# Gate and up of three feed-forwards as seven block products, with weight blocks summed by accumulating DMAs

## The chip, the cores and the metric

The kernel runs on one core of a Trainium2 chip. The metric is device time in microseconds (us), from the start of the program to its end; lower is better. The kernel before takes 2795.41 us (median of 3 runs, 2793.9 to 2799.13).

## What is computed

Two small transformer blocks, one after the other, on 512 tokens of width 1024, all in float32. The first has a hybrid mixer (sparse attention and an mLSTM), a cross-attention and a feed-forward (FFN 0). The second has two layers, each of half-step FFN, mixer, half-step FFN: FFN 1, a conformer convolution and FFN 2 in layer 0, then FFN 3, an attention and FFN 4 in layer 1. The change is in FFN 1, 2 and 4, which are, cut to what matters:

```python
D_MODEL, SEQ, D_FF_2 = 1024, 512, 2816
def swiglu_ffn_2(x, w_gate, w_up, w_down):
    return (jax.nn.silu(x @ w_gate) * (x @ w_up)) @ w_down
...
h = h + HALF_STEP * swiglu_ffn_2(rms_norm_2(h, ffn1_norm[layer]), ffn1_w_gate[layer], ...)
...
h = h + HALF_STEP * swiglu_ffn_2(rms_norm_2(h, ffn2_norm[layer]), ffn2_w_gate[layer], ...)
```

## The kernel before, in words

Activations lie transposed in SBUF, as 8 tiles `x[k]` of 128 features by 512 tokens. Every float32 operand of a large product is split in two float32r parts (`split`, L122): ACT copies it to a hi part (`whi`, `xh`, `hh`), DVE subtracts that to get a lo part (`wlo`, `xl`, `hl`). `mm3` (L170) then issues three matmuls for one 128 by 128 block of weights: hi by hi, hi of the weights by lo of the activations, lo of the weights by hi of the activations. So the third of three is the first that needs the weights' lo part. Each matmul loads its own weights.

`load_w` (L160) loads a 128 by 1024 weight tile by a DMA from SP into `wraw` (3 buffers) and splits it into `whi` and `wlo` (4 buffers each). A buffer of `whi` is free again when PE has done the product that used it.

`ffn` (L304) works in two halves of 11 tiles of F (128 of the 2816 hidden features). For each tile it makes gate and up, 8 blocks of weights times 3 matmuls of 512 tokens each (`projs`, L196), multiplies both by the row of inverse norms `rb`, and keeps silu(gate) times up as `hh`/`hl` (`up`, L308). After 11 tiles, `down` (L325) makes the 8 output tiles from them, and `cb` (L1030, in `half_ffn`, L1027) adds half of each to `x`. With `head=2` (of the three FFNs only FFN 1, before) the first two tiles of F are made in two token halves of 256 (`HALVES`), so that PE can start before all of `x` is normalised.

PSUM has 8 banks, handed out in turn by tag: `mm` 2, `sc` 3, `tr` 2, `po` 1. A scheduler orders the instructions of each engine when the program is built; the engines then work through their queues in that fixed order, each instruction waiting on semaphores for its inputs and its buffers. POOL does some sums of squares and nothing in the middle of an FFN; no DMA is issued on it.

Of the kernel before, what the change touches and what calls it, by code (L numbers as in the profile page):

```python
# [9 lines left out]
F32 = mybir.dt.float32  # L10
# [4 lines left out]
P = 128  # L15
# [10 lines left out]
NSA_H = 8  # L26
BUCKETS = 32
BW = 640
WHOLE = slice(0, S)
HALVES = (slice(0, S // 2), slice(S // 2, S))  # L30

# [17 lines left out]
def kernel(ctx: ExitStack, tc: tile.TileContext, t: dict, out: bass.AP):  # L49
# [9 lines left out]
    def nm(s):  # L59
        uid[0] += 1  # L60
        return f"{s}_{uid[0]}"
# [5 lines left out]
    def ps_tile(tag):  # L67
        return psum.tile([P, 512], F32, tag=tag, bufs=banks[tag], name=nm(tag))
# [5 lines left out]
    def mm_tile():  # L74
        return next_tile("mm")
# [39 lines left out]
    def v(name, j):  # L115
        o = VOFF[name] + j
        return vec[:, o : o + 1]
# [4 lines left out]
    def split(src, hi, lo, scale=None, pieces=1, hp=1):  # L122
        if scale is None:
            w = src.shape[-1] // hp
            for c in range(hp):
                sl = slice(c * w, (c + 1) * w) if hp > 1 else slice(None)
                last_hi[0] = nc.scalar.activation(hi[:, sl], src[:, sl], AF.Copy)  # L127
            w = src.shape[-1] // pieces
            for c in range(pieces):
                sl = slice(c * w, (c + 1) * w) if pieces > 1 else slice(None)  # L130
                nc.vector.tensor_tensor(lo[:, sl], src[:, sl], f32(hi[:, sl]), ALU.subtract)  # L131
        else:
            nc.scalar.activation(hi, src, AF.Copy, scale=scale)
            nc.vector.scalar_tensor_tensor(lo, src, scale, f32(hi), ALU.mult, ALU.subtract)  # L134
# [25 lines left out]
    def load_w(ap, width, raw=None, pieces=1, hp=1):  # L160

        if raw is None:
            raw = wp.tile([P, width], F32, tag="wraw", bufs=3, name=nm("wraw"))
            nc.sync.dma_start(raw, ap)
        hi = wp.tile([P, width], F32R, tag="whi", bufs=4, name=nm("whi"))
        lo = wp.tile([P, width], F32R, tag="wlo", bufs=4, name=nm("wlo"))
        split(raw, hi, lo, pieces=pieces, hp=hp)
        return hi, lo

    def mm3(ps, lh, ll, rh, rl, start, stop):  # L170
        nc.tensor.matmul(ps, lh, rh, start=start, stop=False)  # L171
        nc.tensor.matmul(ps, lh, rl, start=False, stop=False)  # L172
        nc.tensor.matmul(ps, ll, rh, start=False, stop=stop)  # L173


    chain = []
# [2 lines left out]
    def tick():  # L179
        if chain:  # L180
            chain[0][0] -= 1
            if chain[0][0] == 0:
                chain.pop(0)[1]()

    def order_pe():
        pe_order.enter_context(tc.manual_schedule(engines={mybir.EngineType.PE}))

    def free_pe():
        while chain:
            chain.pop(0)[1]()  # L190
        pe_order.close()
# [4 lines left out]
    def projs(sets, xs, ts):  # L196
        for k in range(KT):
            sl = slice(k * P, (k + 1) * P)
            for ps, (hi, lo) in sets:
                mm3(ps[:, ts], hi[:, sl], lo[:, sl], xs[k][0][:, ts], xs[k][1][:, ts], k == 0, k == KT - 1)  # L200
                tick()
# [17 lines left out]

    def inv_rms(state, eps=1e-6, ts=WHOLE, psum_only=False):  # L220

        if not state:
            for j in range(KT):
                square_acc(x[j], j, state, eng=nc.vector)
        sums = rms_sums(state, eps, ts)
        rt, pb = rms_rows(sums, ts)
        if psum_only:
            return rt, pb
        rb = act_p.tile([P, S], F32, tag="rb", bufs=2, name=nm("rb"))[:, : ts.stop - ts.start]
        nc.vector.tensor_copy(rb, pb)  # L230
        return rt, rb

    def inv_rms_chain(state, first, second):

        if not state:
            for j in range(KT):
                square_acc(x[j], j, state, eng=nc.vector)
        got = []

        def finish():  # L240
            rt, pb = rms_rows(got[0], WHOLE)
            rb = act_p.tile([P, S], F32, tag="rb", bufs=2, name=nm("rb"))
            nc.vector.tensor_copy(rb, pb)
            got[:] = [rt, rb]

        chain.append([first, lambda: got.append(rms_sums(state, 1e-6, WHOLE))])
        chain.append([second, finish])
        return got
# [55 lines left out]
    def ffn(fp, xs, st, wg, wu, wd, out_cb, head=0, tail=0, step=None):  # L304


        r = []

        def up(p, pg, pu):
            if not r:  # L310
                r.append(inv_rms(st)[1])
            rb = r[0]
            gr = fp.tile([P, S], F32, tag="gr", bufs=2, name=nm("gr"))
            nc.vector.tensor_tensor(gr, pg, rb, ALU.mult)
            nc.scalar.activation(gr, gr, AF.Silu)
            su = fp.tile([P, S], F32, tag="su", bufs=2, name=nm("su"))
            nc.vector.tensor_tensor(su, pu, rb, ALU.mult)  # L317
            nc.vector.tensor_tensor(su, su, gr, ALU.mult)
            hh = fp.tile([P, S], F32R, tag=f"hh{p}", name=nm("hh"))
            hl = fp.tile([P, S], F32R, tag=f"hl{p}", name=nm("hl"))  # L320
            split(su, hh, hl)
            return hh, hl

        def down(half, n, ws, pd, h, ts=WHOLE):
            for k in range(FH):  # L325
                hi, lo = ws[k // 6]
                sl = slice(k % 6 * P, (k % 6 + 1) * P)
                mm3(pd[:, ts], hi[:, sl], lo[:, sl], h[k][0][:, ts], h[k][1][:, ts], k == 0, k == FH - 1)
                tick()

        for half in range(2):
            h = []
            nh = 0 if half else head
            ws = [[load_w(w[n], D, pieces=4) for w in (wg, wu)] for n in range(nh)]
            pss = [(mm_tile(), mm_tile()) for n in range(nh)]
            for ts in HALVES:
                for n in range(nh):
                    projs(list(zip(pss[n], ws[n])), xs, ts)
            free_pe()
            if nh:  # L340
                order_pe()
                got = inv_rms_chain(st, 4, 6)
                pss.append(tuple(at_tile() for _ in range(2)))
                for ps, w in zip(pss[nh], (wg, wu)):
                    proj(ps, load_w(w[nh], D), xs)
                free_pe()
                r.append(got[1])
            for p in range(FH):
                n = half * FH + p
                if p < len(pss):  # L350
                    pg, pu = pss[p]
                else:
                    g = load_w(wg[n], D)
                    u = load_w(wu[n], D)
                    pg = mm_tile()
                    proj(pg, g, xs)
                    pu = at_tile()
                    proj(pu, u, xs)
                h.append(up(p, pg, pu))

            def load_down(n):
                return [load_w(wd[half, n][:, a * P : b * P], (b - a) * P) for a, b in ((0, 6), (6, FH))]

            nt = tail if half else 0
            for n in range(KT - nt):
                pd = mm_tile() if n % 2 else at_tile()
                down(half, n, load_down(n), pd, h)
                out_cb(half, n, pd, WHOLE)
            ws = {n: load_down(n) for n in range(KT - nt, KT)}
            pds = {n: mm_tile() if n % 2 else at_tile() for n in ws}  # L370
            if nt:
                order_pe()
            for ts in HALVES:
                for n in ws:
                    down(half, n, ws[n], pds[n], h, ts)
                    out_cb(half, n, pds[n], ts)
                if nt and step:
                    step(ts)

# [647 lines left out]
    def half_ffn(xs, st, idx, nxt, head=0, tail=0, step=None, ap=False):  # L1027
        st2, xs2 = {}, []

        def cb(half, n, ps, ts):  # L1030
            last_add[0] = nc.vector.scalar_tensor_tensor(x[n][:, ts], ps[:, ts], 0.5, x[n][:, ts], ALU.mult, ALU.add)
            if half == 1:
                if nxt is not None:
                    xs2.append(split_x(n, nxt))
                square_acc(x[n], n, st2, ts, ap)

        with tc.tile_pool(name=f"fp{idx}", bufs=1) as fp:
            ffn(fp, xs, st, t[f"wg{idx}"], t[f"wu{idx}"], t[f"wd{idx}"], cb, head, tail,
                step and (lambda ts: step(st2, ts)))
        return xs2, st2  # L1040

    xs, st = half_ffn(xs, st, 1, "mix_norm_0", head=2)


    rt, rb = inv_rms(st)
    cs = ExitStack()
    cp = cs.enter_context(tc.tile_pool(name="cp", bufs=1))
# [466 lines left out]
```

## Time and profile before

| what | value |
|---|---|
| median of 3 runs | 2795.41 us |
| the profiled execution, its own time | 2799.96 us |
| its span, first to last instruction | 2798.2 us |
| busy: PE, DVE, ACT, POOL | 98%, 52%, 38%, 12% |
| mean granted TensorE clock | 0.994 |

"Busy" is the share of the span in which the engine works on at least one instruction. Matmuls overlap in the pipeline, so the time that one costs is read from the step between the starts of two, not from its own duration. A row of the timeline has the start, the duration, the engine, the source line and the operation with output and inputs; in brackets stands the idle time before it and what ended that.

### The profile page before, as it was taken

Reading aid. Unit: us, or ns where it says so; the run is one execution under the profiler, and the core shown is the slowest. Engines: PE = TensorE matmul, PEld = TensorE weight load, DVE = VectorE, ACT = ScalarE, POOL = GpSimd, SP = SyncE. Lnnn points to the kernel's source line nnn. Section 1 sums busy time; section 2 is a strip of 40 time slices with the busy share of each in tenths; the row PEclk is TensorE's granted clock in tenths of the full one; section 3 lists DMA queues with packets and bytes.
Section 4 is the critical chain, followed back from the end, with each engine's and each line's share of the span. In section 5 each row is a group of like instructions: output and inputs, shape, how many; then the busy total and the mean of one; then the engine's idle time right before and its main releaser. Section 6 shows DMA issues by size and latency. Waiting matters only on the chain.

```text
span 2798.2 us, 35182 instructions
## 1 busy us (share of the span) xinstructions
PE 2731.0 (98%) x13750; PEld 2252.2 (80%) x13750; DVE 1465.1 (52%) x2270; ACT 1074.5 (38%) x1772; POOL 339.0 (12%) x451
## 2 busy tenths in 40 slices
PE   8999999999999999999899999999999997999998
PEld 6877988888888888885788888898888874788887
DVE  7666564643436434449754344534444489543443
ACT  5676544422334323331333233343223366332223
POOL 0133132200002000012210000100000136200001
PEclk9999999999999999999999999999999999999999
DMA  5312321223222233236332322323232320222322
GB/s 194 105 46 99 114 76 53 93 85 109 98 83 92 91 99 103 82 110 171 83 113 87 102 98 85 111 84 104 82 109 89 107 65 4 83 96 85 107 84 81
DMA packets 86923, 263.19 MB, mean 94 GB/s; under 512 B 9655, under 2 KB 13751, under 8 KB 86756
## 3 DMA queue, kind: packets, MB, share of 16 engines
q1 hardware_dynamic: 85148, 258.42, 29.6%
q10 hardware_dynamic: 1608, 2.52, 0.3%
q8 instruction: 108, 1.77, 0.3%
q14 instruction: 59, 0.48, 0.1%
HBM read 256.60 MB, written 4.30 MB: 93 GB/s over the span
## 4 chain that ended last, share of the span: by engine, by line
PE 79%; DVE 4%; issue 1%; DMA 1%; ACT 1%; POOL 0%; SPq 0%; DVEq 0%; ACTq 0%
PE sc L171 9%; PE sc L172 9%; PE sc L173 9%; PE mm L172 7%; PE mm L173 7%; PE mm L171 7%; PE tr L171 6%; PE tr L172 6%; PE tr L173 6%; PE po L171 3%; PE po L172 3%; PE po L173 3%; DVE wlo L131 1%; PE po L1311 1%; DVE c L1114 1%
## 5 line engine op out<-in xcount | busy, mean ns | idle before, releaser
L127 ACT ACTIVATE whi<-wraw 128x1024 fp32r<-128x1024 f32 (+3 forms) x518 | 492.3, 955 | 1287.4 <-PE sc L172 430.7
L131 DVE TENSOR_TENSOR wlo<-wraw,whi 128x1024 fp32r<-128x1024 f32 (+4 forms) x559 | 581.1, 1049 | 384.4 <-ACT whi L127 383.1
L171 PE MATMUL mm<-xh,whi 128*128 128x512 f32 (+1 forms) x760 | 287.7, 379 | 6.3 <-ACT whi L127 5.9
L172 PE MATMUL mm<-xl,whi 128*128 128x512 f32 (+1 forms) x760 | 286.9, 377 | 5.5 <-DVE xl L134 5.5
L173 PE MATMUL mm<-xh,wlo 128*128 128x512 f32 (+1 forms) x760 | 286.4, 377 | 0.0
L171 PE MATMUL sc<-xh,whi 128*128 128x512 f32 (+1 forms) x696 | 270.1, 388 | 0.0
L172 PE MATMUL sc<-xl,whi 128*128 128x512 f32 (+1 forms) x696 | 269.2, 387 | 0.0
L173 PE MATMUL sc<-xh,wlo 128*128 128x512 f32 (+1 forms) x696 | 269.2, 387 | 0.0
L172 PE MATMUL tr<-xl,whi 128*128 128x512 f32 (+1 forms) x592 | 222.8, 376 | 3.1 <-DVE xl L134 3.1
L171 PE MATMUL tr<-xh,whi 128*128 128x512 f32 (+1 forms) x592 | 223.1, 377 | 0.0
L173 PE MATMUL tr<-xh,wlo 128*128 128x512 f32 (+1 forms) x592 | 222.9, 376 | 0.0
L216 POOL TENSOR_TENSOR sqacc<-sq,sq 128x512 f32<-128x512 f32 (+1 forms) x11 | 16.3, 1486 | 1585.7 <-issue 896.0
L317 DVE TENSOR_TENSOR su<-sc,rb 128x512 f32<-128x512 f32 x80 | 55.3, 691 | 252.6 <-PE sc L173 252.6
L171 PEld LDWEIGHTS mm<-xh,whi 128*128 128x128 f32 x760 | 144.3, 190 | 33.2 <-ACT whi L127 5.9
L172 PEld LDWEIGHTS mm<-xl,whi 128*128 128x128 f32 x760 | 144.2, 190 | 31.9 <-DVE xl L134 7.1
L173 PEld LDWEIGHTS mm<-xh,wlo 128*128 128x128 f32 x760 | 144.2, 190 | 25.1 <-DVE wlo L131 0.3
L171 PEld LDWEIGHTS sc<-xh,whi 128*128 128x128 f32 x696 | 130.7, 188 | 29.6 <-issue 2.5
L173 PEld LDWEIGHTS sc<-xh,wlo 128*128 128x128 f32 x696 | 130.7, 188 | 26.5
L172 PEld LDWEIGHTS sc<-xl,whi 128*128 128x128 f32 x696 | 130.7, 188 | 26.3
L171 PE MATMUL sc<-hh,whi 128*128 128x512 f32 (+1 forms) x352 | 132.6, 377 | 0.0
L172 PE MATMUL sc<-hl,whi 128*128 128x512 f32 (+1 forms) x352 | 132.2, 376 | 0.0
L173 PE MATMUL sc<-hh,wlo 128*128 128x512 f32 (+1 forms) x352 | 132.2, 376 | 0.0
(531 smaller groups left out, 5554.0 us busy)
## 6 DMA issues: line engine op xcount, KB each, us to landing
wraw<-wg SPq DMA_DIRECT2D x110, 512.0 KB, 3.4
wraw<-wu SPq DMA_DIRECT2D x110, 512.0 KB, 3.4
wraw<-wd SPq DMA_DIRECT2D x80, 384.0 KB, 3.0
wraw<-wd SPq DMA_DIRECT2D x80, 320.0 KB, 2.8
wraw<-w_pw SPq DMA_DIRECT2D x24, 512.0 KB, 3.5
wraw<-w_in_f SPq DMA_DIRECT2D x15, 512.0 KB, 4.1
R<-glscr SPq DMA_DIRECT2D x28, 264.0 KB, 5.3
x<-xT SPq DMA_DIRECT2D x16, 256.0 KB, 5.9
```

What stands on the lines that cost most here:

```text
L127: last_hi[0] = nc.scalar.activation(hi[:, sl], src[:, sl], AF.Copy)
L131: nc.vector.tensor_tensor(lo[:, sl], src[:, sl], f32(hi[:, sl]), ALU.subtract)
L171: nc.tensor.matmul(ps, lh, rh, start=start, stop=False)
L172: nc.tensor.matmul(ps, lh, rl, start=False, stop=False)
L173: nc.tensor.matmul(ps, ll, rh, start=False, stop=stop)
L216: eng.tensor_tensor(state["acc"][:, ts], state["first"][:, ts], sq[:, ts], ALU.add)
L317: nc.vector.tensor_tensor(su, pu, rb, ALU.mult)
L1114: nc.vector.scalar_tensor_tensor(d, tap(k), v("w_dw", 31 * j + k), d, ALU.mult, ALU.add)
L1311: nc.tensor.matmul(po[64 * hx : 64 * hx + 64, j * P :], vsh[:, j, c0 : c0 + 64], PTs[hx][:, o : o + n_], start=j == 0, stop=j == NT - 1)
```

## The change

FFN 1, 2 and 4 go through a new function, `ffn_blocks`. Its first four tiles of F are made as before (the first two in token halves, now in all three FFNs). From the fifth on, tiles go in pairs. A pair's gate and up weights are cut in four blocks (2 tiles of F by 2 halves of the 1024 features), the activations in four (2 halves of the features by 2 halves of the tokens). Seven products of sums of blocks give what eight products gave, with 4 k blocks, 256 tokens and two lanes (gate, up) each.

The sums of the activations' blocks are made once per FFN on DVE and ACT (`block_sums`). The sums of the weights' blocks are made anew in every pair: SP loads three blocks, and four times POOL issues two DMAs (gate lane and up lane, 256 KB each) that add another block to a buffer that has already been split. PSUM banks accumulate from product to product, and ACT and DVE copy, add or subtract them into `c1` and `c2`. `down` now runs in three chunks, after 8, 16 and 22 tiles of F, and `cb` multiplies by the norms and adds to `x` in two operations.

```diff
+BLOCKED = {1: "ffn1_norm_0", 2: "ffn2_norm_0", 4: "ffn2_norm_1"}
...
+    CHUNKS = ((0, 4), (4, 8), (8, FT // 2))
...
+        def block_sums(kp):
+            r1, r2, r3, r4 = (raw[q, kp] for q in (1, 2, 3, 4))
+            for kk in range(2):
...
+                nc.vector.tensor_scalar(r1[:, c], x[4 + k][:, HI], g2, None, ALU.mult)
+                nc.vector.scalar_tensor_tensor(r1[:, c], x[k][:, HI], g1, r1[:, c], ALU.mult, ALU.subtract)
+                nc.vector.scalar_tensor_tensor(r2[:, c], x[k][:, LO], g1, r1[:, c], ALU.mult, ALU.subtract)
+                nc.vector.scalar_tensor_tensor(r4[:, c], x[4 + k][:, LO], g2, r2[:, c], ALU.mult, ALU.subtract)
+                nc.vector.tensor_tensor(r3[:, c], x[k][:, LO], x[k][:, HI], ALU.subtract)
+            split(r1, *sums[1, kp])
...
+        def weights(m):
+            def block(q):
+                cols = slice(q // 2 * 512, q // 2 * 512 + 512)
+                return wg[2 * m + q % 2][:, cols], wu[2 * m + q % 2][:, cols]
+            def load(q, tag):
+                w = fp.tile([P, D], F32, tag=tag, bufs=2, name=nm("wb"))
+                for lane, src in enumerate(block(q)):
+                    nc.sync.dma_start(w[:, 512 * lane : 512 * lane + 512], src)
+                return w
+            def add(w, q):
+                for lane, src in enumerate(block(q)):
+                    nc.gpsimd.dma_start(w[:, 512 * lane : 512 * lane + 512], src, accum_op=ALU.add)
+                return w
+            b1 = load(0, "wbt")
+            yield load_w(None, D, b1)
+            b2 = load(2, "wbv")
+            yield load_w(None, D, b2)
+            yield load_w(None, D, add(b1, 1))
+            b3 = load(3, "wbu")
+            yield load_w(None, D, add(b1, 3))
+            yield load_w(None, D, b3)
+            yield load_w(None, D, add(b3, 1))
+            yield load_w(None, D, add(b1, 2))
+        def product(ps, a, w, fresh):
+            hi, lo = w
+            for lane in range(2):
+                for k in range(4):
+                    sl = slice(lane * 512 + k * P, lane * 512 + k * P + P)
+                    mm3(ps[:, lane * 256 : lane * 256 + 256], hi[:, sl], lo[:, sl], a[k][0], a[k][1], ...)
...
+        def pair(m, p):
...
+            product(A, a11, next(ws), True)
+            nc.scalar.activation(of_half(c1, 0), lanes(A), AF.Copy)
+            yield
+            B = ps_tile("sc")
+            product(B, a12, next(ws), True)
+            nc.vector.tensor_tensor(of_half(c1, 0), of_half(c1, 0), lanes(B), ALU.add)
+            yield
+            E = ps_tile("tr")
+            product(E, s1, next(ws), True)
+            nc.scalar.activation(of_half(c2, 1), lanes(E), AF.Copy)
+            yield
+            product(A, s2, next(ws), False)
+            nc.scalar.activation(of_half(c2, 0), lanes(A), AF.Copy)
+            yield
+            product(E, s4, next(ws), False)
+            nc.vector.tensor_tensor(of_half(c2, 0), lanes(E), of_half(c2, 0), ALU.subtract)
+            yield
+            product(A, s3, next(ws), False)
+            nc.vector.tensor_tensor(of_half(c2, 1), of_half(c2, 1), lanes(A), ALU.subtract)
+            act(c2, p + 1)
+            yield
+            product(A, a22, next(ws), False)
+            nc.scalar.activation(of_half(c1, 1), lanes(A), AF.Copy)
+            act(c1, p)
+            yield
...
+            for m in ms:
+                for i in range(5):
+                    next(gens[m])
+                if m + 1 in gens:
+                    next(gens[m + 1])
+                next(gens[m])
...
-        def cb(half, n, ps, ts):
-            last_add[0] = nc.vector.scalar_tensor_tensor(x[n][:, ts], ps[:, ts], 0.5, x[n][:, ts], ALU.mult, ALU.add)
+        def cb(half, n, ps, ts, rb=None):
...
+                yr = fp.tile([P, D], F32, tag="c0", bufs=2, name=nm("yr"))
+                nc.vector.scalar_tensor_tensor(yr[:, ts], ps[:, ts], 0.5, rb[:, ts], ALU.mult, ALU.mult)
+                last_add[0] = nc.vector.tensor_tensor(x[n][:, ts], x[n][:, ts], yr[:, ts], ALU.add)
```

How the order on the engines changes is seen best in the middle of FFN 1. First DVE, before: one tile of F (`gr` and `su` are gate and up out of PSUM, `hl` the lo part of the result), with the copies of the next weights between.

```order
L314 TENSOR_TENSOR gr_1648_8980<-tr_1646_8930,rb_1567_8507 128x512
L131 TENSOR_TENSOR wlo_1666_9065<-wraw_1664_9062,whi_1665_9064 128x1024
L317 TENSOR_TENSOR su_1649_8983<-sc_1647_8955,rb_1567_8507 128x512
L318 TENSOR_TENSOR su_1649_8983<-su_1649_8983,gr_1648_8980 128x512
L131 TENSOR_TENSOR wlo_1669_9071<-wraw_1667_9068,whi_1668_9070 128x1024
L131 TENSOR_TENSOR hl_1651_8987<-su_1649_8983,hh_1650_8986 128x512
```

The same engine and place after the change, in the second pair of the second chunk (`wb_1743` is the buffer of its blocks 0, 1, 3, 2 in turn, `wb_1755` that of its 3 and 1; `wb_1765` and `wb_1771` belong to the next pair; L487, L497 and L500 take PSUM into `c`).

```order
L133 TENSOR_TENSOR wlo_1754_9759<-wb_1743_9654,whi_1753_9758 128x1024
...
L487 TENSOR_TENSOR c_1740_9651<-c_1740_9651,sc_1748_9722 128x2x256
L467 TENSOR_TENSOR c_1720_9452<-c_1720_9452 128x512
L133 TENSOR_TENSOR wlo_1757_9793<-wb_1743_9654,whi_1756_9792 128x1024
L133 TENSOR_TENSOR wlo_1759_9822<-wb_1755_9787,whi_1758_9821 128x1024
L133 TENSOR_TENSOR hl0_1705_9437<-c_1720_9452,hh0_1704_9436 128x512
L497 TENSOR_TENSOR c_1741_9652<-tr_1752_9755,c_1741_9652 128x2x256
L133 TENSOR_TENSOR wlo_1761_9853<-wb_1755_9787,whi_1760_9852 128x1024
L133 TENSOR_TENSOR wlo_1767_9893<-wb_1765_9889,whi_1766_9892 128x1024
L133 TENSOR_TENSOR wlo_1769_9924<-wb_1743_9654,whi_1768_9923 128x1024
L133 TENSOR_TENSOR wlo_1773_9962<-wb_1771_9958,whi_1772_9961 128x1024
```

The lo parts of the sums stand in the order of the products, and the lo part for the sixth product (`wlo_1761`) stands behind L497, which takes the fifth product out of PSUM. In 18 of the 27 pairs it stands so; in the first pair of each chunk it stands ahead of L497.

PE at the same place, from the last matmul of the fifth product (into `tr_1752`) on: two matmuls of the sixth (into `mm_1742`), two of the next pair's first (into `mm_1764`), then the first that needs `wlo_1761`.

```order
L175 MATMUL tr_1752_9755<-sh41_1590_8550,wlo_1759_9822 128x256
L175 MATMUL mm_1742_9653<-sh30_1575_8535,whi_1760_9852 128x256
L175 MATMUL mm_1742_9653<-sl30_1576_8536,whi_1760_9852 128x256
L175 MATMUL mm_1764_9888<-xh0_1102_5431,whi_1766_9892 128x256
L175 MATMUL mm_1764_9888<-xl0_1103_5432,whi_1766_9892 128x256
L175 MATMUL mm_1742_9653<-sh30_1575_8535,wlo_1761_9853 128x256
```

Before, the three matmuls of a block stood together everywhere in this stage. POOL, which had no row there, now has eight DMAs per pair, each behind a wait for DVE's lo part of the buffer it adds to (`DVE`), or for its own lane's earlier DMA (`DMASW`, `DMAHW`):

```order
L439 DMA wb_1743_9654<-wg1 128x512 [waits DMAHW1_49,DVE_49]
L439 DMA wb_1743_9654<-wu1 128x512 [waits DMAHW2_49]
L439 DMA wb_1743_9654<-wg1 128x512 [waits DMASW0_49,DVE_49]
L439 DMA wb_1743_9654<-wu1 128x512 [waits DMASW1_49]
L439 DMA wb_1743_9654<-wg1 128x512 [waits DMASW4_49,DMASW2_49,DVE_49]
L439 DMA wb_1743_9654<-wu1 128x512 [waits DMASW5_49,DMASW3_49]
L439 DMA wb_1755_9787<-wg1 128x512 [waits DMAHW7_49,DMASW6_49,DVE_49]
L439 DMA wb_1755_9787<-wu1 128x512 [waits DMAHW0_49,DMASW7_49]
```

The three sums for the third, fourth and seventh product come first, then the one for the sixth.

## Rows read from the trace of the kernel before

**Rows 1.** The page: span, busy time of each engine, granted clock in 40 slices.
```profile
span 2798.2 us, 35182 instructions
PE 2731.0 (98%) x13750; PEld 2252.2 (80%) x13750; DVE 1465.1 (52%) x2270; ACT 1074.5 (38%) x1772; POOL 339.0 (12%) x451
PEclk9999999999999999999999999999999999999999
```

**Rows 2.** Waits of PE, longest first: engine, line, releaser, us in total, times, longest.
```profile
PE sc L270 <- POOL rt L263: 7.9, 5, 2.7
PE tr L1295 <- DVE PT L1300: 6.8, 6, 1.9
PE mm L171 <- ACT whi L127: 5.9, 1, 5.9
```

**Rows 3.** Windows, FFN 1: length, busy us (instructions) by engine, clock, DMA share, GB/s.
```profile
920.00:1180.00 260.00, 260.00 (x1149) 215.29 (x1148) 109.98 (x134) 72.17 (x89) 0.00 (x0) 1.00 0.30 94
```

**Rows 4.** Timeline of PE in a stream of 512 columns: start, duration, operation.
```profile
1299.88 0.39 PE L172 MATMUL tr<-xl,whi 128*128 128x512 f32 x1
...
1304.19 0.39 PE L173 MATMUL tr<-xh,wlo 128*128 128x512 f32 x1
```

**Rows 5.** Timeline of PE in a stream of 256 columns.
```profile
857.79 0.28 PE L173 MATMUL tr<-hh,wlo 128*128 128x256 f32 x1
...
861.39 0.28 PE L173 MATMUL tr<-hh,wlo 128*128 128x256 f32 x1
```

**Rows 6.** Groups by line and shape: busy us, mean ns of one, idle before.
```profile
L127 ACT ACTIVATE whi<-wraw 128x1024 fp32r<-128x1024 f32 x332 | 350.7, 1060 | 854.7 <-PE sc L172 264.7 <-PE mm L172 191.3 <-PE tr L172 181.1
L131 DVE TENSOR_TENSOR wlo<-wraw,whi 128x1024 fp32r<-128x1024 f32 x317 | 390.2, 1233 | 197.9 <-ACT whi L127 197.0 <-PE tr L1295 0.3
```

**Rows 7.** Timeline of FFN 1: DVE's steps, and the hand-over from PE to DVE.
```profile
939.30 0.69 DVE L318 TENSOR_TENSOR su<-su,gr 128x512 f32<-128x512 f32 x1
939.91 1.22 DVE L131 TENSOR_TENSOR wlo<-wraw,whi 128x1024 fp32r<-128x1024 f32 x1
941.04 0.68 DVE L131 TENSOR_TENSOR hl<-su,hh 128x512 fp32r<-128x512 f32 x1
...
943.51 0.39 PE L173 MATMUL tr<-xh,wlo 128*128 128x512 f32 x1
943.52 0.19 PEld L171 LDWEIGHTS sc<-xh,whi 128*128 128x128 f32 x1
...
943.94 0.69 DVE L314 TENSOR_TENSOR gr<-tr,rb 128x512 f32<-128x512 f32 x1 [2.21 <-PE tr L173]
```

**Rows 8.** DMA issues (KB each, us to landing), one issue on SP, POOL's smallest operation.
```profile
wraw<-wg SPq DMA_DIRECT2D x110, 512.0 KB, 3.4
wraw<-wd SPq DMA_DIRECT2D x80, 384.0 KB, 3.0
wraw<-wd SPq DMA_DIRECT2D x80, 320.0 KB, 2.8
L164 SPq DMA_DIRECT2D wraw<-wg x110: 327/328/328, 465.6 to 2684.4; - x110
L263 POOL TENSOR_TENSOR rt<-ms,nhalf 128x4 f32<-128x4 f32 x10 | 13.9, 1386 | 177.1 <-DVE ms L259 148.2 <-DVE ms L261 28.9
```

**Rows 9.** Start of FFN 1: timeline of PE and DVE, then windows.
```profile
863.36 0.39 PE L172 MATMUL mm<-xl,whi 128*128 128x256 f32 x1 [1.57 <-DVE xl L134]
866.29 0.39 PE L172 MATMUL mm<-xl,whi 128*128 128x256 f32 x1 [1.95 <-DVE xl L134]
883.65 3.08 DVE L218 TENSOR_TENSOR sqacc<-sqacc,sq 128x512 f32<-128x512 f32 x4
888.38 2.36 DVE L131 TENSOR_TENSOR wlo<-wraw,whi 128x1024 fp32r<-128x1024 f32 x2 [1.66 <-ACT whi L127]
893.80 0.39 PE L173 MATMUL po<-xh,wlo 128*128 128x512 f32 x1
...
867.00:868.00 1.00, 1.00 (x10) 1.00 (x8) 1.00 (x3) 0.41 (x1) 1.00 (x2) 0.76 0.84 299
868.00:872.00 4.00, 4.00 (x19) 3.86 (x19) 3.97 (x11) 1.12 (x3) 1.34 (x2) 0.50 0.50 163
872.00:874.00 2.00, 1.49 (x8) 1.20 (x8) 0.65 (x3) 0.00 (x0) 0.88 (x1) 0.50 0.10 39
874.00:876.00 2.00, 2.00 (x17) 2.00 (x17) 1.61 (x6) 0.96 (x3) 1.72 (x3) 0.91 0.00 0
```

More of the change, by code (lines that the diff above doesn't have):

```diff
@@ L168, in load_w, with mm3 @@
         return hi, lo
[L170 to L173, printed above, removed]
+    def mm3(ps, lh, ll, rh, rl, start, stop, more=False):
+        for c, (a, b) in enumerate(((lh, rh), (lh, rl), (ll, rh))):
+            nc.tensor.matmul(ps, a, b, start=start and c == 0, stop=stop and c == 2, skip_group_check=more)
     chain = []
@@ L1028, in half_ffn @@
         st2, xs2 = {}, []
-        def cb(half, n, ps, ts):
-            last_add[0] = nc.vector.scalar_tensor_tensor(x[n][:, ts], ps[:, ts], 0.5, x[n][:, ts], ALU.mult, ALU.add)
+        def cb(half, n, ps, ts, rb=None):
+            if rb is None:
+                last_add[0] = nc.vector.scalar_tensor_tensor(x[n][:, ts], ps[:, ts], 0.5, x[n][:, ts], ALU.mult, ALU.add)
+            else:
+                yr = fp.tile([P, D], F32, tag="c0", bufs=2, name=nm("yr"))
+                nc.vector.scalar_tensor_tensor(yr[:, ts], ps[:, ts], 0.5, rb[:, ts], ALU.mult, ALU.mult)
+                last_add[0] = nc.vector.tensor_tensor(x[n][:, ts], x[n][:, ts], yr[:, ts], ALU.add)
             if half == 1:
@@ L1037, in half_ffn @@
         with tc.tile_pool(name=f"fp{idx}", bufs=1) as fp:
-            ffn(fp, xs, st, t[f"wg{idx}"], t[f"wu{idx}"], t[f"wd{idx}"], cb, head, tail,
-                step and (lambda ts: step(st2, ts)))
+            end = step and (lambda ts: step(st2, ts))
+            if idx in BLOCKED:
+                ffn_blocks(fp, xs, st, BLOCKED[idx], t[f"wg{idx}"], t[f"wu{idx}"], t[f"wd{idx}"], cb, 2, tail, end)
+            else:
+                ffn(fp, xs, st, t[f"wg{idx}"], t[f"wu{idx}"], t[f"wd{idx}"], cb, head, tail, end)
         return xs2, st2
     xs, st = half_ffn(xs, st, 1, "mix_norm_0", head=2)
+    turn.update(mm=["tr", "mm"], at=["sc", "po", "sc", "sc"])
     rt, rb = inv_rms(st)
```

113 lines of the change are left out of this document (added).

## The prediction

> **What bounds the kernel now.** Read the page's head first: TensorE is busy for 98% of the span at full clock [rows 1]. The list of PE's waits then says how much could come from waiting less: its longest entry is 7.9 us in all [rows 2]. So only less TensorE work, or new waits, move the time. The windows view of the first half-step FFN says what stands beside PE: in 260 us PE never idles, DVE is busy for 110, ACT for 72, POOL for none, the DMA engines for 0.30 of it [rows 3]. The timeline gives the step from one matmul to the next: over 19 steps of 512 columns 1304.19 - 1299.88 = 4.31 us, 0.2268 us each [rows 4]; over 30 of 256 columns 861.39 - 857.79 = 3.60, 0.120 each [rows 5]. Every step has its own weight load, so both hold for such streams. All times below are set against the profiled execution, 2799.96 us (span 2798.2), which lies 4.6 above the median 2795.41; I subtract that at the end. A measurement of this kernel can tell about 0.2% (5.6 us) from no change.
>
> **Removed: matmul columns.** F tiles 4 to 21 are 9 pairs in each of three FFNs, 27 pairs. A pair had 2 x 2 x 8 x 3 = 96 matmuls of 512 columns: 96 x 0.2268 = 21.77 us. Now it has 7 x 2 x 4 x 3 = 168 of 256: 168 x 0.120 = 20.16. The columns fall by an eighth, the time by 1.61 us only, because 256 columns cost more than half of 512. 27 x 1.61 = **43.5 us gained**.
>
> [...]
>
> **Added: the sums' chain.** Write p1 to p7 for a pair's products in program order. With the blocks numbered as in `weights`, theirs are 0; 2; 0+1; 0+1+3; 3; 3+1; 0+1+3+2. Each product needs a hi copy on ACT (1.06 us) and then a lo copy on DVE (1.23) [rows 6]; with a hand-over of 0.05 that is 2.34. An accumulating DMA may start only when both have read the buffer, and the next copy only when it has landed. Call L the time from the end of the lo copy to the landing of both 256 KB lanes. In steady state the order on DVE is lo6, next pair's lo1, lo7, ..., lo3, ..., lo4, lo5, ..., lo6. So one pair's chain is: sum (L), 2.34, sum (L), 2.34, lo5 right behind lo4 (a lo copy every 1.14 [rows 7]), sum (L), 2.34, next lo1 behind lo6 (1.14): **3 L + 9.3 us**, against 20.16 of PE.
>
> The first pair of each of the three chunks starts early, behind the down products. There the fifth copy waits for the hi buffer of p1 (four buffers): p1's end at 24 x 0.12 + 0.17 = 3.05, 2.34 later lo5, then L, 2.34 and 0.25 for the weight load: p6 can go on at L + 8.0. PE is there after 124 matmuls, at 14.9. For the n-th pair of a chunk PE has thus waited (n-1)(3L + 9.3 - 20.16) + (L + 8.0 - 14.9) in all.
>
> Even with a small L there is a floor. In the 18 pairs that are not first, DVE's queue holds p5's eviction ahead of lo6, and p6's third matmul needs lo6. From the start of p5's last matmul the eviction starts 0.32 later (matmul 0.28, then 0.04 as at 943.90 to 943.94), lo6 0.61 after it, it takes 1.23, and the load 0.25: 2.41 [rows 5, 7]. PE has four matmuls to fill it, so p6 would be due at 0.60: 1.81 us lost per pair, 18 x 1.81 = 32.6.
>
> **What L is.** The trace has no accumulating DMA and none issued by POOL, so bounds. From below: 320, 384 and 512 KB land 2.8, 3.0 and 3.4 us after their issue on SP [rows 8], which continued to 256 KB is 2.6, and a second lane 0.33 behind makes 2.9. From above: an accumulating lane moves its destination too, so it is like 512 KB, 3.4, and the two lanes run one after the other: 6.8. I take the middle of 3.4 and 6.8, **5.1**: lanes of 512 KB weight that overlap by half. Then 3L + 9.3 = 24.6, the n-th pair of a chunk has waited 4.44 (n-1) - 1.8, and chunks of 2, 3 and 4 pairs lose 2.6, 7.1 and 11.5, 21.2 per FFN, **63.7 us lost** in three. The floor lies inside this (it is the same wait of PE at p6), so it is not added.
>
> **POOL's own queue.** The two issues of p7's sum stand ahead of the two of p6's, whose buffer is ready 1.14 us later. An issue takes 0.33 on SP, POOL's smallest operation 1.39 [rows 8]: halfway, two are 1.72, 0.58 late. 18 pairs x 0.58 = **10.4 lost** (0 to 1.64 x 18 = 30).
>
> **Starts and ends.** FFN 2 and FFN 4 now begin with two F tiles in token halves: 192 x 0.120 - 96 x 0.2268 = 1.27 each, 2.5. The activations' sums put 13 us of work on DVE at each start. In FFN 2 and 4 it lies among the last updates of x, and PE needs the eighth split 80 matmuls (9.6 us) after it starts, so I cost it at nothing. In FFN 1 some 8 us stand ahead of the weights of F tile 2, which are split at 888.38 and due at 893.80, after a DVE that is free at 886.73 [rows 9]: 2 us. At the end of each FFN the update of x is two operations: 0.6 more, three times, 1.8. Together **6.3 lost**. If DVE had no room here, the three starts would cost up to 13 each.
>
> **Cost at nothing.** The down products stay 528 matmuls per FFN. Their evictions become 24 x 2 instead of 16 x 1, 0.61 each, under a DVE that is idle for over half the time [rows 3]. Per pair DVE has 7 x 1.14 + 9 x 0.61 = 13.5 us and ACT 12.3 under 20.16: neither is full, only their order binds. Weight traffic goes from 2.0 to 3.5 MB a pair; 3.5 MB in 24.6 us is 142 GB/s, by [rows 3] 0.45 of the DMA engines, 0.7 if the destinations of the sums count too.
>
> **Sum**: -43.5 + 63.7 + 10.4 + 6.3 = +36.9: 2836.9 profiled, **2832 us** in the median, 1.3% slower.
>
> **Rivals.** R1, *sums in time*: L at or below 4.2, where 3L + 9.3 meets 20.16 + 1.81. Then the floor remains: -43.5 + 32.6 + 6.3 = -4.6, 2791 us; without the starts' costs 2784. For it: the 512 KB row is 3.4 and the DMA engines are idle for 0.7 of the time. Against: two issues on an engine with no such row, and twice the bytes. It decides the sign; chance 0.27. The Trainium skill (DMA: Bandwidth & Descriptors, section Anatomy of one DMA) fits 2.0 us plus bytes/436e3 for one DMA of that path, 2.6 for 256 KB: with the lanes side by side that is R1; no run here shows it yet.
>
> R2, *lanes one after the other*: L = 6.8, 3L + 9.3 = 29.7, the chunks wait 9.4, 19.0 and 28.5, 171 in all: -43.5 + 171 + 10.4 + 6.3 = +144, 2939 us. For it: nothing in the trace shows such transfers overlapping. Chance 0.16.
>
> R3, *the clock falls in the new gaps*: at the start of FFN 1 two PE gaps of 1.57 and 1.95 us were followed by a granted clock of 0.50 (1.2 GHz), by the shares of the windows for 6.8 us [rows 9]. If each later pair's wait of 4.4 us does the same, up to half of 6.8 us is added in 18 pairs: +61 on the forecast, 2893. Against: the waits come in two or three parts, and in a pair bound by the chain a slower PE first uses up its own waiting. Chance 0.12.
>
> **How the numbers follow.** Forecast 0.45, its own range 2804 (L 4.6) to 2876 (L 5.8). The range for 8 in 10 goes from R1 without start costs, 2785, to R2, 2940. Faster: 0.16, R1's better half. Same: 0.11 from R1 and 0.04 from the forecast's low end, 0.15. Slower: 0.69.
>
> **What would show it.** In the timeline of a later pair: about 24.6 us from one p6 to the next, PE waiting for ACT's copy of a sum (p4, p6) or its lo, 4.4 us a pair. POOL's DMA row in the list of DMA issues should land in 4 to 5 us; that row plus the second issue is L. Right on R1 would be PE waiting only at p6, for DVE's lo, 1.8 us, and pairs of 22. Wrong at the root would be 256-column steps off 0.120, waits of PE in the first pairs, or waits in the down products.

## The result, and the profile after

| what | before | after |
|---|---|---|
| median of 4 runs each | 2797.27 us | 3060.26 us (3055.77 to 3063.85) |
| ratio of after to before, 95% interval | | 1.0937 (1.0913 to 1.0961) |
| span of the profiled execution | 2798.2 us | 3058.8 us |
| mean granted TensorE clock | 0.994 | 0.950 |

The change makes the kernel 9.4% slower. The forecast was 2832 us in a range of 2785 to 2940. The side was right; the loss is 260.6 us by the spans, where 36.9 were forecast.

The head of the page after, beside [rows 1]: PE falls from 98% to 92% of the span, and the clock has low slices where the three feed-forwards lie.

```profile
span 3058.8 us, 40423 instructions
...
PE 2814.5 (92%) x15856; PEld 2416.9 (79%) x15856; DVE 1675.8 (55%) x2554; ACT 1212.7 (40%) x1967; POOL 532.4 (17%) x667
...
PEclk9999999999988989899999898999999999998998
```

The waits of the kernel after, longest of each kind (us in total, times, longest), beside [rows 2]. PE waits for ACT's hi copy, ACT for the landing of an up lane, POOL for DVE's lo copy: one ring.

```profile
POOL wb L439 <- DVE wlo L133: 895.8, 80, 47.4
...
ACT whi L129 <- DMA wb<-wu: 378.2, 72, 8.4
...
PE mm L175 <- ACT whi L129: 153.4, 52, 5.9
```

The DMA issues (KB each, us to landing), beside [rows 8]: an accumulating gate lane lands 4.1 us after its issue, an up lane 6.2.

```profile
wb<-wg POOLq DMA_DIRECT2D x108, 256.0 KB, 4.1
wb<-wu POOLq DMA_DIRECT2D x108, 256.0 KB, 6.2
```

The timeline of one round in the second chunk of FFN 1 (start, duration, engine, operation, in brackets the idle time before and what ended it):

```profile
1095.26 1.22 DVE L133 TENSOR_TENSOR wlo<-wb,whi 128x1024 fp32r<-128x1024 f32 x1 [4.68 <-ACT whi L129]
...
1102.79 2.00 ACT L129 ACTIVATE whi<-wb 128x1024 fp32r<-128x1024 f32 x2 [4.44 <-DMA wb<-wu]
...
1103.88 2.36 DVE L133 TENSOR_TENSOR wlo<-wb,whi 128x1024 fp32r<-128x1024 f32 x2 [4.80 <-ACT whi L129]
...
1105.40 0.87 POOL L439 DMA_DIRECT2D wb<-wg  x1 [6.85 <-DVE wlo L133]
1105.94 1.23 POOL L439 DMA_DIRECT2D wb<-wu  x1
...
1106.54 1.54 POOL L439 DMA_DIRECT2D wb<-wg  x1
1107.08 1.89 POOL L439 DMA_DIRECT2D wb<-wu  x1
...
1114.88 3.90 ACT L129 ACTIVATE whi<-wb 128x1024 fp32r<-128x1024 f32 x4 [4.11 <-DMA wb<-wu]
1115.97 4.63 DVE L133 TENSOR_TENSOR wlo<-wb,whi 128x1024 fp32r<-128x1024 f32 x4 [2.17 <-ACT whi L129]
...
1118.63 0.87 POOL L439 DMA_DIRECT2D wb<-wg  x1 [9.66 <-DVE wlo L133]
```

The lo copy of the third product ends at 1096.48, and the hi copy of the fourth starts at 1102.79, when its sum has landed, 6.3 us later. The two lo copies that end at 1106.24 are those of the fourth and fifth product. POOL issues the seventh's sum, then the sixth's. The sixth's has landed at 1114.8, when ACT starts on the next four hi copies: 8.56 us after the lo copy. The next pair's first lo ends at 1118.34, and POOL issues the sum for its third. That is the chain of the prediction with other sizes. Taken like this over all 27 pairs, the round trip L (end of the lo copy to the landing of both lanes) is 7.7 us for the third product, 6.4 for the fourth and 8.5 for the sixth. From one fifth lo copy to that of the next pair it is 32.7 us in the mean of the 18 pairs that follow another. In these 18 intervals the third's L is 8.3 us in the mean (in the first pairs of the chunks it is 6.5, and they lie in no interval), so the three L make 23.2. The other 9.6 us are copies, where 9.3 were forecast.

The clock falls behind this gap, as windows of the same stretch show (length, busy us of PE, PEld, DVE, ACT and POOL, granted clock, DMA share, GB/s): PE idles, then works at 0.50, 1.2 GHz.

```profile
1102.00:1104.00 2.00, 0.10 (x1) 0.10 (x1) 0.12 (x1) 1.21 (x2) 0.00 (x0) 0.77 0.02 2
1104.00:1108.00 4.00, 3.54 (x15) 3.24 (x16) 2.84 (x3) 1.79 (x3) 2.60 (x4) 0.50 0.25 28
```

### The profile page after: what moved, and what is told of

Its sections match the earlier page's. It is cut to its first block, busy times and chain, and to the rows that moved or that the text cites. A ratio compares the mean times of both kernels' runs of the same rounds, so it can differ in the third digit from the quotient of the medians.

```text
span 3058.8 us, 40423 instructions
## 1 busy us (share of the span) xinstructions
PE 2814.5 (92%) x15856; PEld 2416.9 (79%) x15856; DVE 1675.8 (55%) x2554; ACT 1212.7 (40%) x1967; POOL 532.4 (17%) x667
## 4 chain that ended last, share of the span: by engine, by line
PE 52%; DMA 14%; issue 8%; DVE 8%; ACT 3%; POOL 2%; SPq 0%; DVEq 0%; ACTq 0%; POOLq 0%
PE sc L175 16%; PE mm L175 16%; PE tr L175 12%; DMA wb<-wu 12%; PE po L175 5%; DVE wlo L133 4%; ACT whi L129 2%; POOL wb L439 2%; DMA wb<-wg 2%; DVE c L1339 1%; PE po L1536 1%; DVE conv L1339 1%; PE sc L160 1%; PE tr L1520 0%; PE sc L259 0%
## 5 line engine op out<-in xcount | busy, mean ns | idle before, releaser
L133 DVE TENSOR_TENSOR wlo<-wraw,whi 128x1024 fp32r<-128x1024 f32 (+4 forms) x451 | 453.6, 1022 | 278.1 <-ACT whi L129 277.6
L133 DVE TENSOR_TENSOR wlo<-wb,whi 128x1024 fp32r<-128x1024 f32 x189 | 224.3, 1220 | 302.6 <-ACT whi L129 302.6
L129 ACT ACTIVATE whi<-wb 128x1024 fp32r<-128x1024 f32 x189 | 191.1, 1051 | 470.6 <-DMA wb<-wu 378.2
L175 PE MATMUL mm<-xh,whi 128*128 128x256 f32 (+1 forms) x1016 | 340.3, 335 | 35.5 <-ACT whi L129 34.9
L175 PE MATMUL mm<-xl,whi 128*128 128x256 f32 (+1 forms) x1016 | 336.3, 331 | 5.5 <-DVE xl L136 5.5
L175 PE MATMUL mm<-xh,wlo 128*128 128x256 f32 (+1 forms) x1016 | 334.4, 329 | 0.5 <-DVE wlo L133 0.5
L175 PE MATMUL mm<-sh,whi 128*128 128x256 f32 (+1 forms) x448 | 170.9, 382 | 125.3 <-ACT whi L129 118.4
L175 PEld LDWEIGHTS mm<-sh,whi 128*128 128x128 f32 x448 | 122.8, 274 | 136.1 <-ACT whi L129 126.4
L175 PE MATMUL mm<-sh,wlo 128*128 128x256 f32 (+1 forms) x448 | 167.2, 373 | 17.1 <-DVE wlo L133 17.1
L175 PE MATMUL mm<-sl,whi 128*128 128x256 f32 (+1 forms) x448 | 164.0, 366 | 0.0
```

The source lines that it names most:

```text
L175: nc.tensor.matmul(ps, a, b, start=start and c == 0, stop=stop and c == 2, skip_group_check=more)
```

## The experiments

Eleven runs were made. The theory: a later pair lasts as long as three round trips of sums and some 10 us of copies, and what was mis-sized is the round trip. The first rival: PE at half clock, or the evictions, set the pair's time. Round trips and pair times below are read as above and are means over the 27 sums of a kind, and over the 18 later pairs. The kernels of this table were timed once each, but for the kernel after, whose four times lie within 8.1 us. An edit can change the order that the scheduler gives the engines; where it did and it matters, the text says so.

| kernel | L of third, fourth, sixth | pair | time |
|---|---|---|---|
| after | 7.7, 6.4, 8.5 | 32.7 | 3060.3 |
| two of three matmuls | 7.5, 6.1, 8.7 | 32.5 | 3035.5 |
| sixth's sum issued first | 7.1, 6.1, 6.3 | 29.9 | 2971.7 |
| one lane accumulates | 4.5, 4.0, 4.8 | 24.2 | 2847.9 |
| plain copies from POOL | 4.9, 4.0, 4.7 | 24.2 | 2840.5 |
| plain copies from SP | not all known | 22.7 | 2795.0 |
| no adds | none | 20.2 (on PE) | 2770.8 |

**No adds.** The 216 accumulating DMAs are taken out.

```diff
             def add(w, q):
-                for lane, src in enumerate(block(q)):
-                    nc.gpsimd.dma_start(w[:, 512 * lane : 512 * lane + 512], src, accum_op=ALU.add)
                 return w
```

> The changed kernel without the 216 accumulating DMAs: the sums of the weights' blocks are left out, everything else (copies, products, evictions, loads) stays. Theory of the chain (a pair's time is three round trips of sums plus 10 us of copies): the chain is gone, pairs fall from 33 us to 20.2 to 22, total 2765 to 2795 us. Rival, the waits come from evictions, the order on DVE or the granted clock and not from the sums: pairs stay above 28 us, total above 2930.

Measured: 2770.8 us in one run, beside 2799.6 for the kernel before. The products, evictions and activations' sums cost little by themselves; 289 us hang on the accumulating DMAs and on the order that the scheduler gives with them. From one third product to the next PE takes 20.16 us in all 18 later pairs, and it has no gap in the second chunk of FFN 1 (a window, as above):

```profile
1015.40:1084.40 69.00, 69.00 (x578) 69.00 (x577) 46.85 (x52) 38.68 (x50) 0.00 (x0) 1.00 0.26 85
```

**Two of three matmuls.** The hi by lo matmul of every block in the seven products is dropped.

```diff
-                    mm3(ps[:, lane * 256 : lane * 256 + 256], hi[:, sl], lo[:, sl], a[k][0], a[k][1], ...)
+                    nc.tensor.matmul(ps2, hi[:, sl], a[k][0], start=first, stop=False, ...)
+                    nc.tensor.matmul(ps2, lo[:, sl], a[k][0], start=False, stop=end, ...)
```

> In the seven products the second of the three matmuls (hi of the weights by lo of the activations) is left out: a pair has 112 matmuls instead of 168, 13.4 us of PE at full clock. Theory of the chain: PE is not in the cycle of a later pair, pairs stay at 33 us, the total falls by 0 to 60 (first pairs and ends of chunks only), 3000 to 3060. Rival, PE at half clock after each gap sets the pair's time: the total falls by 27 x 56 x 0.12 = 181 us or more, to 2880 or less.

Measured: 3035.5 us. A third of PE's work in the pairs is gone, and a later pair is 32.5 us long instead of 32.7. PE waits longer instead, as its list of waits shows (L460 is that kernel's line of the first matmul):

```profile
PE mm L460 <- ACT whi L129: 247.8, 64, 7.4
```

So neither PE's work nor its clock is in the cycle of a later pair. From the third product of a first pair to the first down product of its chunk the nine chunks take 749 us here and 742 after, so the 25 us that did go lie ahead of those stretches: PE comes to the third product some 2.5 us sooner after the down products.

**Plain copies from POOL.** The same DMAs in the same order on every engine, without the addition.

```diff
-                    nc.gpsimd.dma_start(w[:, 512 * lane : 512 * lane + 512], src, accum_op=ALU.add)
+                    nc.gpsimd.dma_start(w[:, 512 * lane : 512 * lane + 512], src)
```

> The same DMAs from the same queue in the same order, but plain copies instead of accumulating ones (the sums are left out). Theory A, the read and add at the destination is what makes a lane land 6.2 us after its issue: lanes land in 3.5 us, a round trip is about 4.4 in place of 7.8, a pair 23 us, total about 2830. Theory B, POOL's queue is what costs, whatever the DMA does: landing as before, pairs of 33 us, total 3040 to 3060.

Measured: 2840.5 us, and pairs of 24.2. The DMA issues of this kernel, to be set beside 4.1 and 6.2 after:

```profile
wb<-wg POOLq DMA_DIRECT2D x108, 256.0 KB, 3.0
wb<-wu POOLq DMA_DIRECT2D x108, 256.0 KB, 3.3
```

PE, DVE and ACT have the order of the kernel after, so nothing but the addition differs: it costs 220 us, theory A. In the 18 intervals the round trips of this kernel make 14.2 us (5.4, 4.0 and 4.7), and my formula gives 14.2 + 9.3 = 23.5 for a pair.

The prediction also had a floor: PE loses 1.81 us at the sixth product of every later pair however small L is, 32.6 in all, because its lo copy stands behind L497. This run keeps that order. In 17 of the 18 pairs PE waits for the sixth's hi copy first, and the floor can't be told apart. In the last pair of the second chunk of FFN 2 it does not, and the timeline shows the step from the fifth's last matmul to the sixth's third:

```profile
1659.68 0.28 PE L175 MATMUL tr<-sh,wlo 128*128 128x256 f32 x1
...
1660.07 0.69 DVE L497 TENSOR_TENSOR c<-tr,c 128x512 f32<-128x512 f32 x1 [5.68 <-PE tr L175]
...
1661.95 0.39 PE L175 MATMUL mm<-sh,wlo 128*128 128x256 f32 x1 [1.75 <-DVE wlo L133]
```

It is 2.27 us, where 2.41 were forecast.

**Plain copies from SP.** The same, issued by SP.

```diff
-                    nc.gpsimd.dma_start(w[:, 512 * lane : 512 * lane + 512], src, accum_op=ALU.add)
+                    nc.sync.dma_start(w[:, 512 * lane : 512 * lane + 512], src)
```

> Like the run with plain copies on POOL's queue, but on SP's queue (the sums are left out, the order on DVE and PE is nearly that run's). If POOL's queue by itself costs anything, round trips fall below the 4.0 to 4.9 us of that run and the total below its 2840, to 2800 to 2825; if the two queues are alike, 2830 to 2850; if waits on SP hold up the loads queued behind them, above 2850.

Measured: 2795.0 us, 45 less than from POOL's queue and lower than I expected. POOL's queue has a price of its own: from the third product's lo copy to the start of the fourth's hi copy it is 3.6 us here and 4.3 from POOL. How much of the 45 that is stays open. The scheduler put the lo copy of the sixth product ahead of L497 in all 18 later pairs, where from POOL it stands behind it, which the prediction prices at up to 1.81 us a pair.

**One lane accumulates.** The gate lane's sums are left out; the up lane's stay.

```diff
-                for lane, src in enumerate(block(q)):
+                for lane, src in list(enumerate(block(q)))[1:]:
                     nc.gpsimd.dma_start(w[:, 512 * lane : 512 * lane + 512], src, accum_op=ALU.add)
```

> Each sum adds the up lane alone, by one accumulating DMA of 256 KB; the gate lane's sums are left out. Theory (two lanes run one after the other, about 2.2 us each at the destination): a round trip alone falls from 6.4 to about 4.1 us, that of the sixth, behind the seventh's one lane, from 8.5 to about 5, the third's to 4.8; a pair is 13.9 + 10.1 = 24 us and the total 2830 to 2860. Rival, the cost is in each accumulating DMA by itself and the lanes overlap: round trips stay above 6 us, the total above 2990.

Measured: 2847.9 us, pairs of 24.2. A single accumulating lane lands 3.7 us after its issue where nothing is ahead of it (the fourth product's). In the kernel after the same sum's two lanes land 3.8 us and 6.1 us after the first issue, though the issues are 0.54 apart. So a second lane lands some 2.3 us behind the first. The DMA issues of this kernel, over all four sums:

```profile
wb<-wu POOLq DMA_DIRECT2D x108, 256.0 KB, 4.1
```

Four lanes, the seventh's two and then the sixth's, land in the order of their issue, 4.2, 6.5, 8.1 and 9.4 us after the first one in the mean of the kernel after. The last two steps are 1.6 and 1.3 us and not 2.3: the lanes queue, but not strictly one after the other.

**Sixth's sum issued first.** POOL's queue keeps the program's order in the pairs.

```diff
-            next(gens[ms[0]])
-            for m in ms:
+            with tc.manual_schedule(engines={mybir.EngineType.Pool}):
+                next(gens[ms[0]])
+                for m in ms:
...
```

> POOL's queue is held in the program's order in the pairs, so the add for the sixth product is issued ahead of the one for the seventh. Theory (the sixth's two lanes wait behind the seventh's two): the sixth's round trip falls from 8.5 to 6.4 us, a pair from 33 to about 30.5, total 2995 to 3020. Rival, all lanes share one rate, so what the sixth wins the next pair's third loses: no change, 3045 to 3060.

Measured: 2971.7 us, 88 less than after, more than expected. The sixth's round trip falls from 8.5 to 6.3, and the third's from 7.7 to 7.1. The DMA issues, beside 4.1 and 6.2 after:

```profile
wb<-wg POOLq DMA_DIRECT2D x108, 256.0 KB, 3.8
wb<-wu POOLq DMA_DIRECT2D x108, 256.0 KB, 5.5
```

The later pairs, 2.8 us shorter, make 50 of the 88; 28 more lie in the first pairs and the ends of the chunks. The order on DVE changed too (the sixth's lo copy stands behind L497 in 7 of the 18 later pairs), so 88 us is the price of the order on POOL's queue with what the scheduler made of it. I had put 10.4 us on it.

**Sums on POOL.** Block 1 is loaded by SP as well, and the sums are tensor adds in SBUF.

```diff
-                for lane, src in enumerate(block(q)):
-                    nc.gpsimd.dma_start(w[:, 512 * lane : 512 * lane + 512], src, accum_op=ALU.add)
+                nc.gpsimd.tensor_tensor(w, w, other, ALU.add)
...
+            b4 = load(1, "wraw", wp, 3)
-            yield load_w(None, D, add(b1, 1))
+            yield load_w(None, D, add(b1, b4))
...
```

> Block 1 is loaded by SP too, and the four sums are tensor adds on POOL in SBUF instead of accumulating DMAs (2.0 MB of loads per pair, as before the change; full computation). Theory of the chain: a round trip is one POOL add of about 3 us instead of 7.8, three of them plus 10 are 19, under 20.2 of PE; the gain of 43.5 remains but for the starts' 6 to 20: 2765 to 2780, faster than both. Rival: POOL's adds and DVE's copies slow each other, adds of 5 us or more, pairs of 25 us and more, total above 2860.

Measured: 2841.2 us, ratio 1.0143 (1.0126 to 1.0160); a pair takes 24. The expectation fell, and the rival's mechanism holds, though an add stays at 2.6 us in the mean. The groups of this kernel show the price on DVE, 1598 ns for a lo copy that is 1220 in the kernel after:

```profile
L133 DVE TENSOR_TENSOR wlo<-wb,whi 128x1024 fp32r<-128x1024 f32 x189 | 299.3, 1598 | 77.5 <-ACT whi L129 77.4
...
L438 POOL TENSOR_TENSOR wb<-wb,wb 128x1024 f32<-128x1024 f32 x108 | 280.6, 2599 | 620.4 <-DVE wlo L133 538.1
```

Its timeline shows single operations. DVE's product of 128x512 (L466) beside a POOL add lasts 2.12 us instead of 0.69, and its lo copy 3.04 instead of 1.23:

```profile
1086.80 0.68 DVE L486 TENSOR_TENSOR c<-c,sc 128x512 f32<-128x512 f32 x1
1087.39 3.04 DVE L133 TENSOR_TENSOR wlo<-wb,whi 128x1024 fp32r<-128x1024 f32 x1
...
1091.74 2.12 DVE L466 TENSOR_TENSOR c<-c 128x512 f32<-128x512 f32 x1 [0.70 <-ACT c L465]
...
1086.96 2.39 POOL L438 TENSOR_TENSOR wb<-wb,wb 128x1024 f32<-128x1024 f32 x1 [2.43 <-DVE wlo L133]
1090.52 2.79 POOL L438 TENSOR_TENSOR wb<-wb,wb 128x1024 f32<-128x1024 f32 x1 [1.17 <-DVE wlo L133]
```

The two engines take turns: 13.5 us of DVE and 4 x 2.4 of POOL make 23.1, and the pair has 24. In the trace one or both of them are busy for 21.3 us of a later pair in the mean, so turns explain most of the pair, not all. The Trainium skill (SBUF — State Buffer, section Who interferes with whom) says that a DVE instruction with two SBUF inputs contends with a GpSimd instruction that reads SBUF. These rows agree; the operation before, L486, which takes one input from PSUM, kept its 0.68.

**Sums on DVE.** The same adds on DVE.

```diff
-                nc.gpsimd.tensor_tensor(w, w, other, ALU.add)
+                nc.vector.tensor_tensor(w, w, other, ALU.add)
```

> The four sums as tensor adds on DVE in place of POOL (block 1 loaded by SP, full computation). In the run with adds on POOL DVE's operations took 2.1 and 3.0 us beside an add instead of 0.7 and 1.2: the two take turns, and 13.5 + 4 x 2.4 = 23.1 us of turns made a pair of 24. On DVE an add is 1.14: 13.5 + 4.6 = 18.1, under 20.2 of PE. Theory: pairs of 20.2 to 21, total 2765 to 2785, faster than both kernels. Rival: DVE at 90% in a fixed order delays evictions and copies, pairs of 22.5 and more, total 2810 or more.

Measured: 2770.5 us, ratio 0.9905 (0.9890 to 0.9920), 1% faster than the kernel before. The sixth's lo copy stands ahead of the fifth product's eviction in all 18 later pairs, so it is not delayed by it. A window over the later pairs of a chunk and the down products behind them shows PE without a gap at full clock, DVE at 76%:

```profile
1040.00:1120.00 80.00, 80.00 (x544) 74.53 (x544) 60.88 (x71) 36.11 (x46) 0.00 (x0) 1.00 0.38 121
```

And the first matmul of the third product in two pairs after each other is 20.16 us apart, 168 x 0.120, the price that the prediction took from [rows 5]:

```profile
1013.42 0.28 PE L175 MATMUL tr<-sh,whi 128*128 128x256 f32 x1
...
1033.58 0.28 PE L175 MATMUL tr<-sh,whi 128*128 128x256 f32 x1
```

**Seventh's sum by DMA.** As the last, but the seventh product's sum stays with the accumulating DMA.

```diff
-            yield load_w(None, D, add(b1, b2))
+            for lane, src in enumerate(block(2)):
+                nc.gpsimd.dma_start(b1[:, 512 * lane : 512 * lane + 512], src, accum_op=ALU.add)
+            yield load_w(None, D, b1)
```

> As the run with sums on DVE, but the seventh product's sum stays an accumulating DMA: it is needed four products (11.5 us) after the fourth's copy, and a round trip alone is 6.4 and the copies 2.3. Theory: an accumulating DMA with that much slack costs nothing, and DVE has 17.0 us per pair: the same as the run with all sums on DVE or up to 5 us faster, 2760 to 2785. Rival: the DMA disturbs the loads or the order, more than 10 us slower than that run.

Measured: 2788.8 us, ratio 0.9966 (0.9951 to 0.9980), 18 us slower than with all sums on DVE. The rival holds. The last pair of FFN 1's second chunk shows how in the timeline:

```profile
1077.69 0.87 POOL L451 DMA_DIRECT2D wb<-wg  x1 [17.29 <-DVE wlo L133]
1078.24 1.22 POOL L451 DMA_DIRECT2D wb<-wu  x1
...
1085.35 1.06 ACT L129 ACTIVATE whi<-wb 128x1024 fp32r<-128x1024 f32 x1 [3.47 <-DMA wb<-wu]
1086.31 0.58 ACT L492 ACTIVATE c<-tr 128x512 f32<-128x512 f32 x1
...
1086.94 0.39 PE L175 MATMUL tr<-sh,whi 128*128 128x256 f32 x1 [3.02 <-ACT c L492]
```

The hi copy stands at the head of ACT's queue until the lanes land, the third product's eviction L492 stands behind it, and the fifth waits 3.02 us for the bank. PE's waits of this kind in the whole program (us in total, times, longest):

```profile
PE tr L175 <- ACT c L492: 7.7, 3, 3.0
```

That is part of the 18 us; the rest was not traced. My slack counted the seventh product alone and not what is queued behind its copy.

**Sums after the norms.** The version with sums on DVE; in FFN 1 the activations' sums read a copy of the norm's weights that depends on the inverse norms.

```diff
+        gate = vec[:, o : o + KT]
+        if gname == "ffn1_norm_0":
+            gate = fp.tile([P, KT], F32, name=nm("gate"))
+            nc.vector.scalar_tensor_tensor(gate, r[0][:, :KT], 0.0, vec[:, o : o + KT], ALU.mult, ALU.add)
...
-                g1, g2 = v(gname, k), v(gname, 4 + k)
+                g1, g2 = gate[:, k : k + 1], gate[:, 4 + k : 5 + k]
```

> The version with the weights' sums on DVE, and in FFN 1 the activations' sums wait for the norms (they read a copy of the norm's weights that is made from the inverse norms), so that they no longer stand between the sums of squares on DVE. Theory (the 6.6 us wait of PE for the sums of squares at FFN 1's start, and the half clock behind it, come from that order): the wait goes, 6 to 11 us faster than the run with sums on DVE (2770.5), 2760 to 2765. Rival, the sums made later hold up the evictions of the first F tiles or the first pair: no gain or a loss, 2768 to 2780.

> The version with sums on DVE once more, for the comparison on the same chip: 2766 to 2775, ratio 0.989 to 0.992.

Measured on one chip: 2764.3 us, ratio 0.9873 (0.9858 to 0.9887), and 2771.0 for the version without this edit, ratio 0.9897 (0.9881 to 0.9914). The wait it aims at is in the list of PE's waits with sums on DVE:

```profile
PE sc L259 <- DVE sqacc L220: 6.6, 1, 6.6
```

The kernel after has it too. PE stands until DVE has added the last squares, and the windows behind it are at half clock:

```profile
904.59 0.34 PE L259 MATMUL sc<-ones,sqacc 128*128 128x1 f32 x1 [5.70 <-DVE sqacc L220]
...
906.00:908.00 2.00, 2.00 (x6) 1.71 (x7) 0.16 (x1) 0.00 (x0) 1.02 (x1) 0.50 0.09 35
908.00:910.00 2.00, 2.00 (x6) 1.52 (x6) 0.00 (x0) 0.00 (x0) 0.00 (x0) 0.50 0.00 0
```

With the edit the same stretch has no gap and full clock:

```profile
895.00:915.00 20.00, 20.00 (x116) 17.61 (x115) 17.09 (x35) 9.37 (x15) 1.02 (x1) 1.00 0.12 38
```

## Why the prediction was right and where it was wrong

**Right: what was removed.** Pairs of 20.16 us were seen where the sums don't bind. 43.5 gained and 6.3 lost at starts and ends would make 37.2; the last version, whose sums are on DVE and which has no stall at the start of FFN 1, is 36.0 shorter than before by the spans (2762.2 against 2798.2).

**Right: the chain.** Which three sums follow each other, that the seventh's is not among them, and that PE is not in the cycle, all came out. The copies between are 9.6 us instead of 9.3. With the three L as measured in the later pairs the formula gives 23.2 + 9.3 = 32.5, and the pair has 32.7.

**Wrong: "What L is".** The step that failed is the size of L: 5.1 us for every sum, where 6.4, 7.7 and 8.5 were measured. Two lanes with nothing ahead of them take 6.4, below my upper bound of 6.8 but near it: the second lands 2.3 us behind the first, and I had chosen "lanes that overlap by half". The other two sums lie beyond the bound, since it counted a sum's own two lanes and nothing else on the queue. The sixth's lanes stand behind the seventh's two; putting them first brought 8.5 down to 6.3. The third's round trip is 6.5 us in the first pairs of the chunks and 8.3 in the others, where SP's loads for the next pair fall beside it. That the loads do it is read from the trace and was not tried by itself. In the later pairs the three errors add 7.9 us, and a wait that grows by the pair is paid in all 18: 18 x (32.7 - 20.16) = 226 us, where 18 x 4.44 = 80 was in the sum.

**Wrong: "POOL's own queue".** I charged the order of the issues with the issue time, 0.58 us in a pair. What the order costs is the lanes' time ahead: 2.2 us in the sixth's round trip, and 88 us in all in the run that changed it.

**First pairs and ends.** I gave each chunk 1.8 us in hand. It was the other way: PE waits at the sixth product in all nine first pairs, 0.6 to 5.0 us. Take the stretch from the first matmul of the third product to the first down product. In the second chunk of FFN 1 it is 116.5 us after, and 72.1 with the sums on DVE; the three later pairs explain 39.1 of the 44.4 between. Over all nine chunks it is 742 us, and the 3866 matmuls in it need 464 at 0.120 each. Of the 278 lost, 226 lie in the later pairs and 52 in the first pairs and ends, where the sum had 16 in hand. By the run with two of three matmuls (749 us) PE and its clock do not set them; the longer L of the sixth does in part, and the rest stays open.

With 278 in place of 63.7 and 10.4 the sum is +241, and +260.6 was measured. FFN 1's start explains some 5 of the difference; the others were not traced.

**Not shown: the floor as a sum.** R1's 2791 us rests on the 32.6 us that a small L would still lose. The step of 2.41 was seen once, as 2.27; the 32.6 were not. Without adds and with sums on DVE the scheduler put the sixth's lo copy ahead of the fifth's eviction in all 18 pairs, and PE never waited there. One sum of the prediction is off as well: its formula gives 2801 us for L 4.6, not 2804. Nothing rests on it.

**Starts.** 2 us were put on FFN 1, with 13 as the bound. PE waited 5.70 us and then worked at half clock; taking the cause away won 6.6 us. The order on DVE was the cause; I had looked at the weights of F tile 2 and had let the sums of squares through for free.

**The rivals.** R2 was nearest, with lanes in series and 2939 us: a sum's own two lanes come close to that (6.4 of 6.8), and the queue ahead of the sixth's lanes took it further. R1 asked for L at or below 4.2, and the plain copies show what that means: with round trips of 4.0 to 4.9 the time was 2840, and by SP, in another order, 2795. By the Trainium skill's fit (DMA: Bandwidth & Descriptors, section Anatomy of one DMA) the estimate is 2.6 us for 256 KB; plain lanes from POOL took 3.0 and 3.3, an accumulating one 3.7 alone, which the fit does not speak of. R3 saw the clock fall as these traces show it, but in the later pairs a slower PE only used up its own waiting, which was the argument against it: with a third of PE's work gone the pair stayed at 32.5.

## What to carry to other kernels

Where a buffer is read, changed and read again, cost the loop as a chain of round trips, and price each by everything that is ahead of it on its queue, not by the transfer alone. A range for a cost that recurs in a chain has to be widened for every pair that it is paid in. A sum of two small tiles that an engine with idle time can make in 1.2 us should not be a DMA of 6 us in a loop of 20, and which engine has room depends on what it shares: POOL was idle here, and DVE, with less room, was the better place.

## What was not expected of the hardware

Two accumulating DMAs of 256 KB, issued 0.54 us apart on POOL's queue, land 3.8 and 6.1 us after the first issue; as plain copies they land 2.9 and 3.7 after it. With four in the queue the third and fourth follow 1.6 and 1.3 us behind the one before. POOL's busy time for an issue rises as well, from 0.55 to 0.87 us and more. DVE's operations on two SBUF inputs last up to 2.5 and 3.1 times as long beside a POOL add of 128x1024 (1.23 to 3.04, 0.69 to 2.12), while POOL's own adds take 2.6 us in the mean.
